# Loads in their order of use, an early table load and four products of zeros at the start of a decoder step on one core

## The chip, the core and the metric

The kernel runs on one core of a Trainium2 chip. Each engine works through its own list of instructions in order: TensorE (PE, with its weight loads as PEld), VectorE (DVE), ScalarE (ACT), GpSimd (POOL) and SyncE (SP), which here only issues loads and stores. An engine stops at an instruction until the semaphores that it waits for have come, and everything behind that instruction on the same engine stops too. The metric is the device time of one execution, in microseconds (us); lower is better.

## The reference, cut to what matters

One decoder layer takes a prompt of 1024 positions and 8 x 8 new positions of running sequences, 1088 columns of 1024 features in all. It has two parts, a token mixer (gated convolution, dilated attention, grouped attention) and a SwiGLU feed-forward network. Each part first norms its input and modulates it by a conditioning vector:

```
mod = silu(c) @ w_mod + b_mod              # c: 9 vectors of 1024; six groups of 1024 values
shift1, scale1, gate1, shift2, scale2, gate2 = split(mod, 6)
h   = rmsnorm(x, g_mix) * (1 + scale1) + shift1
... = h @ w_in                             # 1024 -> 2560 columns, read by all head groups
x   = x + gate1 * (mix @ w_out)
x   = x + gate2 * swiglu(rmsnorm(x, g_ffn) * (1 + scale2) + shift2, ...)
y   = rmsnorm(x, norm_final)
```

The change lies in the first microseconds of this: `silu(c)`, the first parts of `mod`, and the first projections of `h`.

## The kernel before

Data lie transposed: features on the 128 partitions, positions along the free dimension. So x is eight tiles x0 to x7 of 128 x 1088 (544 KB each), and the 1088 columns are worked in three groups of 366, 366 and 356. A product with full precision is made of three fast ones (lines 204, 205 and 206): every operand is cut into a high and a low part of the type fp32r, and high x high, high x low and low x high are added up in PSUM. For weights the cut is made in `halves` (line 90 on ACT for the high part, line 91 on DVE or POOL for the low part).

The start of the program is one long stage, in which four things run into each other:

- **The modulation.** `csil` is silu of the conditioning vectors (line 153, ACT). The weights `w_mod` come in tiles m0 to m23, four loads of 256 KB each. `mod_tile` (lines 173 to 197) makes two groups of four products of plain fp32 from such a tile (line 179; each of the four writes its own 32 of the 128 partitions). Then ACT copies the sum out of PSUM (`modev`, line 184), PE adds the four parts up by two small products (line 186), and DVE writes the result to `MOD` (lines 192 and 195). The tiles m0, m1, m2 and m3 give the scales of x0/x1, x2/x3, x4/x5 and x6/x7; m4 to m7 give the shifts. PSUM bank `t` serves m0 and m2, bank `o` serves m1 and m3; `o` has one buffer.
- **The scaled input.** For each of the eight x tiles ACT writes the high part of x times its scale (line 299) and DVE the low part (line 300), for three column groups.
- **The first two projections.** For each x tile PE makes 18 products (two blocks of weights x three column groups x three kinds), 144 in all, into six banks of PSUM that stay open for the whole stage. Their weights are w0 (for x0 to x3) and w1 (for x4 to x7), each two loads of 256 KB into `eraw`.
- **The norm.** ACT squares each x tile (lines 267 and 270), DVE or POOL adds the squares into `acc` (line 271), PE sums `acc` over the partitions (line 276, nine products of one column), a short chain on DVE and ACT makes the reciprocal root (lines 233 to 239), and PE spreads it over the partitions (line 282).

After line 282 the projections are scaled by the norm and the rest of the layer follows: further projections, attention, the decode part that streams the caches, the feed-forward network.

The order of the loads is written by hand, as a string of names at line 252; SP issues them in that order. At most eight loads of SP and ACT are under way, since they share eight semaphores. The order of the instructions on the other engines is not written by hand: a scheduler places them at build time by its own estimate of when each would be ready. When an input of that estimate changes (an arrival, an instruction more), it may place the instructions of all engines anew.

An fp32 product shows as two records in the trace, so that the four products of one group of line 179 are "x8" there and x4 in the program.

## Time and profile before

| what | value |
|---|---|
| three runs | 1392.35, 1392.99 and 1393.65 us, median 1392.99 us |
| the profiled execution: own time | 1396.23 us |
| the profiled execution: span, first to last instruction | 1394.2 us |
| busy share of PE over the span | 97% |
| mean granted clock of PE | 0.984 |
| share of PE in the chain that ended last | 88% |

The profiled execution is 3.2 us above the median of the runs, and its span is 2.0 us shorter than its own time. A timeline row gives the start in us from the span's start, the time in us, the engine, the line, the operation with what it writes and reads, and the count; in brackets the idle time before it and what ended that idle time. A row of windows gives for a stretch the busy time of each engine with its count of instructions, the granted clock of PE, the busy share of the DMA engines and GB/s.

### The profile page before, as it was taken

Reading aid. Unit: us, or ns where it says so; the run is one execution under the profiler, and the core shown is the slowest. Engines: PE = TensorE matmul, PEld = TensorE weight load, DVE = VectorE, ACT = ScalarE, POOL = GpSimd, SP = SyncE. Lnnn points to the kernel's source line nnn. Section 1 sums busy time; section 2 is a strip of 40 time slices with the busy share of each in tenths; the row PEclk is TensorE's granted clock in tenths of the full one; section 3 lists DMA queues with packets and bytes.
Section 4 is the critical chain, followed back from the end, with each engine's and each line's share of the span. In section 5 each row is a group of like instructions: output and inputs, shape, how many; then the busy total and the mean of one; then the engine's idle time right before and its main releaser. Section 6 shows DMA issues by size and latency. Waiting matters only on the chain.

```text
span 1394.2 us, 23856 instructions
## 1 busy us (share of the span) xinstructions
PE 1345.8 (97%) x9097; PEld 1281.3 (92%) x9097; DVE 850.7 (61%) x2016; ACT 596.0 (43%) x1227; POOL 199.1 (14%) x283
## 2 busy tenths in 40 slices
PE   7999999999999997999999999999999999999994
PEld 5889999988898886888999999999999999999994
DVE  4558868356676436325669766666666656566666
ACT  5488875466765324232345323232322222222252
POOL 2042310211101000000010111111111111111114
PEclk9999999999999998999999999999999999999996
DMA  9343431353406669775444413141423232323103
GB/s 362 111 154 100 144 100 32 122 183 107 145 24 228 225 237 333 249 297 182 115 136 123 128 61 91 57 155 61 153 90 129 88 125 91 122 92 121 52 23 129
DMA packets 77187, 190.90 MB, mean 137 GB/s; under 512 B 14048, under 2 KB 23808, under 8 KB 76288
## 3 DMA queue, kind: packets, MB, share of 16 engines
q1 hardware_dynamic: 73376, 135.67, 29.8%
q10 hardware_dynamic: 3536, 53.65, 10.7%
q8 instruction: 72, 1.18, 0.3%
q14 instruction: 43, 0.35, 0.1%
q0 software_dynamic: 160, 0.04, 0.0%
HBM read 181.32 MB, written 59.33 MB: 173 GB/s over the span
## 4 chain that ended last, share of the span: by engine, by line
PE 88%; DMA 4%; DVE 3%; ACT 2%; issue 2%; POOL 1%; SPq 0%; POOLq 0%; ACTq 0%; DVEq 0%
PE ps_g L204 20%; PE ps_g L206 19%; PE ps_g L205 19%; PE ps_s L205 3%; PE ps_s L204 3%; PE ps_s L206 3%; PE ps_o L582 3%; PE ps_t L204 2%; PE ps_t L205 2%; PE ps_t L206 2%; PE ps_t L573 2%; DMA wraw<-in_w_gu 2%; PE ps_s L529 1%; PE ps_s L530 1%; PE ps_g L179 1%
## 5 line engine op out<-in xcount | busy, mean ns | idle before, releaser
L204 PE MATMUL ps_g<-act,wsp 128*128 128x366 f32 (+1 forms) x1192 | 396.5, 334 | 2.2 <-DVE u L327 0.9
L205 PE MATMUL ps_g<-act,wsp 128*128 128x366 f32 (+1 forms) x1192 | 396.0, 332 | 0.0
L206 PE MATMUL ps_g<-act,wsp 128*128 128x366 f32 (+1 forms) x1192 | 392.9, 332 | 0.5 <-DVE wsp L91 0.3
L90 ACT ACTIVATE wsp<-wraw 128x512 fp32r<-128x512 f32 x232 | 145.8, 630 | 273.0 <-PE ps_g L206 174.9
L91 DVE TENSOR_TENSOR wsp<-wraw,wsp 128x512 fp32r<-128x512 f32 x232 | 167.2, 722 | 151.1 <-ACT wsp L90 145.5
L204 PEld LDWEIGHTS ps_g<-act,wsp 128*128 128x128 f32 x1192 | 225.3, 189 | 9.9 <-issue 3.3
L205 PEld LDWEIGHTS ps_g<-act,wsp 128*128 128x128 f32 x1192 | 225.7, 189 | 4.2 <-issue 2.3
L206 PEld LDWEIGHTS ps_g<-act,wsp 128*128 128x128 f32 x1192 | 224.7, 189 | 4.7 <-issue 3.1
L204 PE MATMUL ps_g<-hid,wsp 128*128 128x366 f32 (+3 forms) x464 | 153.6, 333 | 4.6 <-DVE ts L772 3.3
L205 PE MATMUL ps_g<-hid,wsp 128*128 128x366 f32 (+3 forms) x464 | 152.8, 329 | 1.5 <-DVE hid L857 1.4
L206 PE MATMUL ps_g<-hid,wsp 128*128 128x366 f32 (+3 forms) x464 | 153.1, 330 | 0.0
L204 PEld LDWEIGHTS ps_g<-hid,wsp 128*128 128x128 f32 x464 | 88.2, 190 | 7.8 <-DVE cv L768 3.8
L90 ACT ACTIVATE wsp<-tw 128x512 fp32r<-128x512 f32 x64 | 40.5, 633 | 122.2 <-PE ps_g L206 59.0
L205 PEld LDWEIGHTS ps_g<-hid,wsp 128*128 128x128 f32 x464 | 88.4, 191 | 2.3 <-DVE hid L857 2.1
L205 PE MATMUL ps_s<-act,wsp 128*128 128x366 f32 x272 | 90.2, 332 | 0.0
L204 PE MATMUL ps_s<-act,wsp 128*128 128x366 f32 x272 | 90.2, 331 | 0.0
L206 PE MATMUL ps_s<-act,wsp 128*128 128x366 f32 x272 | 90.0, 331 | 0.0
L206 PEld LDWEIGHTS ps_g<-hid,wsp 128*128 128x128 f32 x464 | 88.4, 190 | 0.0
L768 DVE SCALAR_TENSOR_TENSOR p_q<-ps_g,MOD,p_q 128x366 f32<-128x366 f32 (+3 forms) x99 | 55.4, 570 | 42.3 <-PE ps_g L206 42.2
L768 DVE SCALAR_TENSOR_TENSOR p_qc<-ps_g,MOD,p_qc 128x366 f32<-128x366 f32 (+3 forms) x99 | 56.5, 572 | 39.4 <-PE ps_g L206 37.6
L976 POOL TENSOR_TENSOR tw<-wraw 128x512 f32<-128x512 f32 x16 | 21.3, 1334 | 347.2 <-DMA wraw<-in_w_gu 209.5
L543 ACT ACTIVATE Sb<-Sb,st 128x257 f32<-128x257 f32 (+5 forms) x96 | 60.5, 632 | 21.1 <-DVE st L535 20.3
(337 smaller groups left out, 2319.3 us busy)
## 6 DMA issues: line engine op xcount, KB each, us to landing
wraw<-in_w_gu SPq DMA_DIRECT2D x112, 256.0 KB, 2.7
wraw<-in_wmod SPq DMA_DIRECT2D x64, 256.0 KB, 3.7
raw<-in_bk SPq DMA_DIRECT2D x30, 512.0 KB, 7.5
raw<-in_bv SPq DMA_DIRECT2D x30, 512.0 KB, 8.0
wraw<-in_w_in SPq DMA_DIRECT2D x36, 256.0 KB, 4.8
wraw<-in_w_d SPq DMA_DIRECT2D x36, 256.0 KB, 2.6
mraw<-in_wmod SPq DMA_DIRECT2D x32, 256.0 KB, 5.2
wraw<-in_w_out SPq DMA_DIRECT2D x32, 256.0 KB, 2.7
```

Source lines behind the costliest of these rows:

```text
L90: S.activation(sp[:, 0, :], raw, AF.Copy)
L91: (V if not state["sub"] or state["n"] % state["sub"] else G).tensor_tensor(sp[:, 1, :], raw, sp[:, 0, :].bitcast(F32), op=OP.subtract)
L179: ins = PE.matmul(ps[32 * q:32 * q + 32, :256], lhsT=csil[:, 4 * hf + q, :], rhs=raws[2 * hf + q // 2][:, q % 2 * 256:q % 2 * 256 + 256], ...
L204: PE.matmul(ps[:, :n], lhsT=w_hi, rhs=a(0, ak), start=first and j == 0, stop=False, **kw)
L205: PE.matmul(ps[:, :n], lhsT=w_hi, rhs=a(1, ak), start=False, stop=False, **kw)
L206: PE.matmul(ps[:, :n], lhsT=w_lo, rhs=a(0, ak), start=False, stop=last and j == m - 1, **kw)
L529: PE.matmul(ps[:, :sn], lhsT=QH[:, qsl], rhs=KS[hd][:, kk], start=True, stop=False)
L543: S.activation(Sb[:, :ne], Sb[:, :ne], AF.Exp, scale=-1.0, bias=m, accum_out=st[:, 3:4])
L573: PE.transpose(pt[:, col:col + 128], Sb[:, (kb - k0) * 128:(kb - k0 + 1) * 128], ident)
L582: PE.matmul(po[:, q0:q0 + w], lhsT=Vt[:, kb, hd].rearrange("p a b -> p (a b)"), rhs=PT[:, hl, c0:c0 + w], start=fresh, stop=ch is chunks[- ...
L768: ins = V.scalar_tensor_tensor(x1[m][:, c0:c0 + k], ps[:, :k], MOD[:, gate + m, 0:1], x1[m][:, c0:c0 + k], op0=OP.mult, op1=OP.add)
L976: G.tensor_tensor(t1, b12, b11, op=OP.subtract)
```

## The change

It has three parts.

1. A tile `warm` of 128 x 256 is set to zero by DVE, and ACT runs Silu on one column of `ones` into its first column, ahead of the instruction that makes `csil`. The table of Silu, which ACT loads before the first instruction that needs it, is so loaded ahead of that instruction; before, the load stood behind the wait for `cT`, the conditioning vectors.
2. Four fp32 products of 128 x 128 by 128 x 256 of that tile lead on PE, into bank `o`, whose values nobody reads. They read the whole tile, the column that ACT writes too, so they wait for ACT's Silu.
3. The loads of the start come in another order.

```
+WARM = 4
 ...
     csil = cse.tile([128, KC, 32], F32, name="csil")
     V.memset(csil, 0.0)
+
+    warm = stp.tile([128, 256], F32, name="warm")
+    V.memset(warm, 0.0)
+    S.activation(warm[:, 0:1], ones, AF.Silu)
+    pw = ps_tile("o")
+    for i in range(WARM):
+        PE.matmul(pw[:, :256], lhsT=warm[:, 128:256], rhs=warm, start=True, stop=True)
     S.activation(csil[:, :, 0:9], cT, AF.Silu)
 ...
-    for item in "m0 w0 m1 x0 x1 m2 x2 m3 x3 x4 w1 x5 x7 x6 m4 m5 m6 m7".split():
+    for item in "m0 x0 w0 x1 m1 x2 x3 m2 x4 w1 x5 m3 x6 x7 m4 m5 m6 m7".split():
```

The lines behind the insertion have numbers higher by 2, then by 9: line 90 becomes 92, 179 becomes 188, 184 becomes 193, 186 becomes 195, 204 to 206 become 213 to 215, 276 becomes 285, 299 becomes 308.

The scheduler answers with another order on every engine in the first 50 us. Beyond, a stretch of some 200 instructions on PE between the last attention and the first decode steps differs in the places of single products, and so do two instructions at the end: the last group's norm is begun by line 233 on DVE and line 234 on ACT, and these now stand behind the three multiplications of line 1077 (DVE) and behind two stores of the output (ACT). Everything else keeps its order.

First place: SP, the very first loads (`mraw` are the tiles m, `eraw` w0 and w1, x_82 to x_89 are x0 to x7). Before:

```order
L97 DMA mraw<-in_wmod 128x512 x4
L97 DMA eraw<-in_w_in 128x512 x2
L97 DMA mraw<-in_wmod 128x512 x4
L257 DMA x_82<-in_xT 128x1088
L257 DMA x_83<-in_xT 128x1088
L97 DMA mraw<-in_wmod 128x512 x4
L257 DMA x_84<-in_xT 128x1088
L97 DMA mraw<-in_wmod 128x512 x4
L257 DMA x_85<-in_xT 128x1088
L257 DMA x_86<-in_xT 128x1088
```

Now:

```order
L99 DMA mraw<-in_wmod 128x512 x4
L266 DMA x_82<-in_xT 128x1088
L99 DMA eraw<-in_w_in 128x512 x2
L266 DMA x_83<-in_xT 128x1088
L99 DMA mraw<-in_wmod 128x512 x4
L266 DMA x_84<-in_xT 128x1088
L266 DMA x_85<-in_xT 128x1088
L99 DMA mraw<-in_wmod 128x512 x4
L266 DMA x_86<-in_xT 128x1088
L99 DMA eraw<-in_w_in 128x512 x2
L266 DMA x_87<-in_xT 128x1088
L99 DMA mraw<-in_wmod 128x512 x4
```

x0 has moved ahead of w0 and m1, and m3 from ahead of x3 to behind x5.

Second place: ACT, from the table load on. Before:

```order
L153 ACT_TABLE_LOAD
L153 ACTIVATE csil<-cT 128x8x9
L90 ACTIVATE wsp<-eraw 128x512
L184 ACTIVATE modev<-ps_t 128x256
L90 ACTIVATE wsp<-eraw 128x512
L184 ACTIVATE modev<-ps_o 128x256
L299 ACTIVATE act<-x_82,MOD 128x366 x2
```

Now:

```order
L158 ACT_TABLE_LOAD
L158 ACTIVATE warm<-ones 128x1
L162 ACTIVATE csil<-cT 128x8x9
L276 ACTIVATE acc_228<-x_82 128x1088
L92 ACTIVATE wsp<-eraw 128x512 x2
L193 ACTIVATE modev<-ps_t 128x256
L308 ACTIVATE act<-x_82,MOD 128x366 x2
```

The copy of m0's sum (`modev<-ps_t`) has moved behind the square of x0 and behind both conversions of w0.

Third place: PE, where m3 is made (`ps_o<-mraw`). Before, after four of its products further up:

```order
L179 MATMUL ps_o<-mraw,csil 32x256
L205 MATMUL ps_g<-act,wsp 128x366
L206 MATMUL ps_g<-act,wsp 128x366
L205 MATMUL ps_s<-act,wsp 128x366
L206 MATMUL ps_s<-act,wsp 128x366
L179 MATMUL ps_o<-mraw,csil 32x256
L204 MATMUL ps_g<-act,wsp 128x356
L204 MATMUL ps_t<-act,wsp 128x356
L179 MATMUL ps_o<-mraw,csil 32x256 x2
L186 MATMUL ps_t<-sel,modev 128x9 x2
L205 MATMUL ps_g<-act,wsp 128x356
```

Now, for its second group of four:

```order
L213 MATMUL ps_t<-act,wsp 128x356
L214 MATMUL ps_t<-act,wsp 128x356
L215 MATMUL ps_t<-act,wsp 128x356
L188 MATMUL ps_o<-mraw,csil 32x256 x4
L195 MATMUL ps_o<-sel,modev 128x9 x2
L285 MATMUL ps_o<-ones,acc_228 128x1 x9
L213 MATMUL ps_g<-act,wsp 128x366
L213 MATMUL ps_s<-act,wsp 128x366
```

The pieces of m3 have become whole groups of four, and the second group, the two products of line 186 (now 195) that need its copy from ACT, and the nine of line 276 (now 285) follow each other with no other product between them; before, other products stood between these three.

## The prediction

> **What bounds the kernel now.** I read the page first: who is busy, and when.
>
> ```profile
> PE 1345.8 (97%) x9097; PEld 1281.3 (92%) x9097; DVE 850.7 (61%) x2016; ACT 596.0 (43%) x1227; POOL 199.1 (14%) x283
> PE   7999999999999997999999999999999999999994
> ```
>
> TensorE works nearly all the time, so a microsecond taken from its list is a microsecond gained, and one that is put in is lost. The change touches the first slice, which has a 7. Two windows of that stretch, and rows of PE's timeline in it, come next.
>
> ```profile
> 10.00:20.00 10.00, 9.18 (x46) 6.21 (x47) 6.78 (x19) 7.53 (x15) 0.51 (x1) 1.00 1.04 402
> 13.74:48.35 34.61, 34.61 (x203) 29.75 (x204) 25.11 (x59) 24.34 (x48) 6.40 (x3) 1.00 0.84 307
> 8.70 1.02 PE L186 MATMUL ps_t<-sel,modev 128*128 128x9 f32 x4 [0.61 <-ACT modev L184]
> 9.88 1.08 PE L179 MATMUL ps_o<-mraw,csil 128*32 128x256 f32 x8 [0.15 <-DMA mraw<-in_wmod]
> 13.74 0.65 PE L204 MATMUL ps_g<-act,wsp 128*128 128x366 f32 x1
> 48.35 0.83 PE L282 MATMUL ps_o<-ident,ir_y 128*128 128x128 f32 x6
> ```
>
> The second row matters most: from the first projection product at 13.74 us to line 282 at 48.35 us PE is busy 34.61 of 34.61 us. Before 13.74 it waits for loads and makes the tiles m0 and m1 meanwhile, so these cost nothing. The time can only fall if the dense stretch begins earlier, holds less work or runs at a faster pace.
>
> Its pace is not even:
>
> ```profile
> 15.10 0.51 PE L205 MATMUL ps_g<-act,wsp 128*128 128x366 f32 x1
> 15.40 0.51 PE L206 MATMUL ps_g<-act,wsp 128*128 128x366 f32 x1
> 17.84 0.50 PE L204 MATMUL ps_t<-act,wsp 128*128 128x356 f32 x1
> 19.28 0.43 PE L205 MATMUL ps_g<-act,wsp 128*128 128x356 f32 x1
> 20.71 0.33 PE L205 MATMUL ps_g<-act,wsp 128*128 128x366 f32 x1
> 20.88 0.33 PE L206 MATMUL ps_g<-act,wsp 128*128 128x366 f32 x1
> ```
>
> A product starts every 0.305 us until 17.84 and every 0.167 us from 19.28 on. The granted clock reads 1.00 in the window from 10 to 20 us above, so it does not show this first slow stretch; the spacing does. The 14 products from 13.74 to 17.84 lose 14 x 0.138 = 1.9 us.
>
> **The table load.** Before:
>
> ```profile
> 3.95 1.28 ACT L153 ACT_TABLE_LOAD   x1 [3.95 <-DMA cT<-in_cT]
> 5.24 0.27 ACT L153 ACTIVATE csil<-cT 128x72 f32<-128x72 f32 x1
> 7.01 1.08 PE L179 MATMUL ps_t<-mraw,csil 128*32 128x256 f32 x8 [0.37 <-DMA mraw<-in_wmod]
> ```
>
> Now the load can run from 2.1 us, when ACT's three DMA issues are over, and `csil` is ready at about 4.2 instead of 5.5. But the second group of m0 starts at 7.01 on its own load, not on `csil`. The gain is zero.
>
> **The zeros.** They wait for ACT's Silu, so they start at about 3.6. Each fills the array as the four products of a group of line 179 do together, and such a group takes 1.08 us at the slow pace, a little less in a stream; four zeros take about 3.8 us (estimate from that row). They end near 7.4, when m0's last load has landed. Cost: at most 0.4 us on m0, covered by ACT's queue below. PE then works without a pause from 3.6 to about 9.4. What they may buy is the fast pace; see the rivals.
>
> **The start of the dense stretch.** It needs x0, w0 and m0's scale.
>
> ```profile
> 12.60 0.23 DVE L296 TENSOR_TENSOR tsx<-x,MOD 128x64 f32<-128x64 f32 x1 [2.06 <-DMA x<-in_xT]
> 9.82 0.48 DVE L192 TENSOR_SCALAR MOD<-ps_t,biasT,gT 128x9 f32<-128x9 f32 x2 [0.64 <-ACT wsp L90]
> 12.71 1.51 ACT L299 ACTIVATE act<-x,MOD 128x366 fp32r<-128x366 f32 x3
> 14.11 1.10 ACT L267 ACTIVATE acc<-x 128x1088 f32<-128x1088 f32 x1
> 8.55 0.62 ACT L90 ACTIVATE wsp<-eraw 128x512 fp32r<-128x512 f32 x1
> 8.28 0.37 ACT L184 ACTIVATE modev<-ps_t 128x256 f32<-128x256 f32 x1
> ```
>
> x0 landed at 12.5 us. At 402 GB/s (the window 10 to 20) a load of 256 KB takes 0.65 us; x0 now passes six of them (w0 and m1), so it lands near 12.5 - 3.9 = 8.6, and w0 at 9.3 and 9.9. This looks like 4 us gained, but ACT's queue takes most of it back: the square of x0 (1.10) and both conversions of w0 (0.62 each) stand ahead of m0's copy. 8.6 + 1.1 = 9.7, two conversions to 10.9, copy to 11.25. Before, line 186 began at 8.70 and its first result could be used about 1.4 later (9.82 plus one of the two writes). So line 299 starts at 12.65 and the first product at 13.2: **0.5 us gained**.
>
> **What the dense stretch holds now.** m1's two groups and its line 186 ran in the idle time before; now they stand inside. m3 was scattered over single products, now it is two whole groups.
>
> ```profile
> 27.05 0.32 PE L206 MATMUL ps_t<-act,wsp 128*128 128x356 f32 x1
> 27.30 0.63 PE L179 MATMUL ps_o<-mraw,csil 128*32 128x256 f32 x6
> 27.86 0.44 PE L204 MATMUL ps_g<-act,wsp 128*128 128x366 f32 x1
> 29.14 0.33 PE L204 MATMUL ps_s<-act,wsp 128*128 128x366 f32 x1
> 29.41 0.62 PE L179 MATMUL ps_o<-mraw,csil 128*32 128x256 f32 x2
> 29.95 0.43 PE L205 MATMUL ps_g<-act,wsp 128*128 128x366 f32 x1
> 33.66 0.54 PE L186 MATMUL ps_o<-sel,modev 128*128 128x9 f32 x4
> ```
>
> Three products of line 179 take 27.86 - 27.05 - 0.167 = 0.64 us out of the stream, and a single one takes 29.95 - 29.14 - 0.167 = 0.64 as well: the four of a group run side by side, and a piece costs the same however few are in it. Line 186 takes about 0.5 (33.66). So m1 adds 2 x 0.64 + 0.5 = **1.8 us**; m3 loses its three pieces too many, of which one lay beside m2's group and cost about a half, 2.5 x 0.64 = **1.6 us** less.
>
> **New waits.** Before, the trace shows none in this stretch. Now PE's list has three places where a result is used right behind its making. (a) m1's line 186, one group of m2, then the products of x2: write of MOD, line 299 and PE's start need about 1.45 us from line 186's start, the work between fills 1.1; wait 0.4. (b) m2's line 186 after only four products of x2, while ACT makes three of line 299 (1.51) and the copy (0.37) first; wait 0.4. (c) m3's second group, copy, line 186, then line 276, which writes the one buffer of bank `o` and waits for DVE's reading of it: 0.2 + 0.37, then 0.3; together 0.9. Sum **1.7 us**, between 0 (each result there in time) and 2.7 (a full microsecond more for ACT being late).
>
> Order and waits together: -0.5 + 1.8 - 1.6 + 1.7 = **+1.4 us**. This takes the slow pace at the start as equally long after the first product.
>
> **A fall of the pace at (c).** Two places in the trace show the clock fall after a thin stretch, and one shows it hold:
>
> ```profile
> 63.60:67.00 3.40, 2.48 (x29) 1.70 (x27) 0.86 (x5) 0.48 (x2) 0.27 (x2) 1.00 0.00 0
> 67.00:70.40 3.40, 3.39 (x30) 3.02 (x31) 0.32 (x2) 0.83 (x4) 0.13 (x1) 0.51 0.00 0
> 364.00:367.40 3.40, 2.24 (x19) 1.46 (x19) 3.22 (x10) 3.34 (x8) 0.00 (x0) 1.00 0.87 270
> 367.40:370.80 3.40, 3.40 (x16) 3.40 (x17) 3.14 (x11) 3.36 (x7) 0.00 (x0) 0.50 0.42 151
> 43.38 2.06 PE L276 MATMUL ps_o<-ones,acc 128*128 128x1 f32 x18
> ```
>
> With 2.48 and 2.24 us of 3.40 busy the next 3.4 us run at half clock. The 2.06 us of one-column products at 43.38 alone did not do it. Now (c) makes group, wait, line 186, wait and line 276 follow each other: 0.64 + 0.57 + 0.5 + 0.3 + 1.9 = 3.9 us without a projection product, thinner than 63.60 to 67.00. I hold a fall for likely. Price: 3.4 us at half pace are 11 products instead of 20, 9 x 0.167 = 1.5 us, less where part of it falls on line 276; I take **+1.0**, bounds 0 and 3.0 (two such windows).
>
> The Trainium skill (TensorE: Matmul & The Clock Gate, "The HAM clock gate") gives that clock a window of about 3.4 us, free-running: one busy window releases it, an idle one halves it. The 3.4 us at 0.51 agree. Its table "Why this matters for your kernels" asks for no idle gap over about 3 us; by that no fall comes at (c), where the longest gap is 0.6 us. The row 63.60 speaks against it.
>
> **Further on.** Between 440 and 472 us, where single products are swapped, PE is full, so the swaps cost nothing, give or take 0.5. At the end the norm waits behind line 1077 today:
>
> ```profile
> 440.00:472.00 32.00, 32.00 (x295) 28.75 (x298) 15.25 (x43) 12.09 (x27) 4.15 (x18) 1.00 0.58 194
> 1379.90 0.52 ACT L1070 ACTIVATE rs<-ps_s 128x416 f32<-128x416 f32 x1 [1.78 <-PE ps_s L806]
> 1380.54 0.16 DVE L233 TENSOR_SCALAR ir_v<-ps_t 128x2 f32<-128x2 f32 x1 [1.83 <-PE ps_t L802]
> 1380.62 0.64 DVE L1077 SCALAR_TENSOR_TENSOR cv<-cv,gT,ps_s 128x416 f32<-128x416 f32 x1
> 1382.29 0.16 DVE L235 RECIPROCAL ir_y<-ir_y 128x2 f32<-128x2 f32 x1
> ```
>
> Their input is there at 1379.9, so in front of line 233 they end at 1381.6 instead of 1382.3; line 233 and ACT's root follow to about 1382.0: **-0.3**, no worse than +0.3.
>
> **Sum.** +1.4 + 1.0 - 0.3 = +2.1 us. The profiled execution's own time, 1396.23, would become 1398.3; it lies 3.2 above the median of the runs. On the median 1392.99 it gives **1395.1 us**.
>
> **Rivals.** *The order alone* (the clock holds at (c)): +1.4 - 0.3, 1394.1. For it: the longest gap there is short. Against: row 63.60.
>
> *The zeros bring the full pace and it lasts.* Then the 1.9 us of the first products, about 0.4 on m1's group and 0.5 on line 186 go. The square of x4 stands on ACT ahead of x2's scaling and waits for x4 (near 20.8: m3's four loads less and one x more than x3 before, at 22.0), so PE's products of x2 can't start before 22.5. In the forecast they start at 13.2 + 36 x 0.167 + 2.3 of slow pace + four groups at 0.64 + 0.5 + wait 0.4 = 25.0, so the gain is at most 2.5: 1.4 - 2.5 - 0.3, 1391.6. For it: 5.8 us of unbroken work; by the skill's budget of about 3.4 us (same page) that suffices. Against: then comes a pause of some 2 us and another of 1 us around a thin line 186, thinner than the rows that lost the clock.
>
> *Faster:* the full pace and no wait at (a), (b), (c), because the scheduler's estimate was right: 1391.6 - 1.7, 1389.9. Against: ACT's chain above.
>
> *Slower still:* the pace falls at (a)-(b) and at (c), each time for two windows: 1.4 + 4 x 1.0 - 0.3, 1398.1. It decides once the waits at (a) and (b) together exceed the 0.9 us idle of the stretch at 63.60.
>
> **How the numbers follow.** Forecast 0.41, order alone 0.25, full pace 0.14, faster 0.06, slower still 0.14. About 0.2% or 2.8 us is what a measurement here tells from no change. Slower by that: the last case, and the part of the forecast with over a full window of half clock, 0.16: 0.30. Faster by that: 0.06 and a part of the full pace, 0.03: 0.09. Within: 0.61. The range runs from just under the full pace to the last case, 1391.2 to 1398.0; the forecast's own is 1393.5 to 1397.
>
> **What would show it.** Line 299's first row near 12.6 and the first product near 13.2; the copy of m0 behind two conversions; waits of PE for ACT's `modev` before lines 195 and 285; half clock in the window behind line 285; line 282's twin later than 48.35. I am wrong if products are 0.167 apart from the first on, if the first stands before 12.5, or if line 282's twin comes earlier than 48.

## The result: slower by 10 us, and the profile after

| | before | after |
|---|---|---|
| median of the runs (eight each) | 1393.10 us (1389.29 to 1399.17) | 1403.36 us (1398.92 to 1407.47) |
| ratio, 95% interval | 1 | 1.0069 (1.0050 to 1.0088) |
| the profiled execution, own time | 1396.23 us | 1401.78 us |
| its span | 1394.2 us | 1399.7 us |

The change makes the kernel slower. The direction was the one forecast, the size was not: 1395.1 was forecast, with a range that ended at 1398.0. The two profiled executions differ by 5.5 us only, since that of before lies 3.1 above its median and that of after 1.6 below. The first rows of after's page:

```profile
PE 1345.0 (96%) x9105; PEld 1282.2 (92%) x9105; DVE 853.3 (61%) x2017; ACT 595.9 (43%) x1228; POOL 201.8 (14%) x283
PE   7999999999999997999999999999999999999994
PEclk9999999999999998999999999999999999999998
```

and the clock's row on the page of before:

```profile
PEclk9999999999999998999999999999999999999996
```

The sums of busy time are those of before within 3 us on every engine, so what has grown is the time in which PE waits. PE's sum could stay the same, although products at half clock take longer, because this execution of before had half clock elsewhere: in its last slice the clock reads 6, in that of after 8. Rows of PE's timeline of after, in the order of the steps of the prediction:

```profile
3.71 3.77 PE L161 MATMUL ps_o<-warm 128*128 128x256 f32 x8 [3.71 <-ACT warm L158]
7.42 1.07 PE L188 MATMUL ps_t<-mraw,csil 128*32 128x256 f32 x16
10.84 1.02 PE L195 MATMUL ps_t<-sel,modev 128*128 128x9 f32 x4 [2.35 <-ACT modev L193]
12.94 0.67 PE L213 MATMUL ps_g<-act,wsp 128*128 128x366 f32 x1 [1.07 <-ACT act L308]
13.40 0.51 PE L213 MATMUL ps_s<-act,wsp 128*128 128x366 f32 x1
13.84 1.08 PE L188 MATMUL ps_o<-mraw,csil 128*32 128x256 f32 x8
14.85 0.68 PE L213 MATMUL ps_g<-act,wsp 128*128 128x366 f32 x1
24.93 0.43 PE L213 MATMUL ps_g<-act,wsp 128*128 128x366 f32 x1 [0.52 <-ACT act L308]
34.75 0.44 PE L214 MATMUL ps_g<-act,wsp 128*128 128x366 f32 x1 [1.16 <-DVE act L309]
37.97 0.44 PE L214 MATMUL ps_g<-act,wsp 128*128 128x366 f32 x1 [1.11 <-DVE act L309]
39.05 0.43 PE L214 MATMUL ps_g<-act,wsp 128*128 128x356 f32 x1 [0.48 <-DVE act L313]
43.63 0.61 PE L195 MATMUL ps_o<-sel,modev 128*128 128x9 f32 x4 [0.59 <-ACT modev L193]
44.98 3.97 PE L285 MATMUL ps_o<-ones,acc 128*128 128x1 f32 x18 [0.74 <-DVE tsx L305]
56.18 0.83 PE L291 MATMUL ps_o<-ident,ir_y 128*128 128x128 f32 x6
```

Down to 24.93 this is the forecast (25.0), in part by luck: the first product is 0.3 us earlier than forecast and fewer products run slowly, while m1's pieces cost more. Then come three waits for DVE, of 1.16, 1.11 and 0.48 us, that no step of the prediction names. Line 285 takes 3.97 us where it took 2.06, and the twin of line 282, the marker of all that follows, starts at 56.18 instead of 48.35: 7.8 us late.

What DVE does ahead of those waits, and POOL beside it (after):

```profile
12.91 3.00 DVE L309 SCALAR_TENSOR_TENSOR act<-x,MOD,act 128x366 fp32r<-128x366 f32 x6
30.34 8.52 DVE L309 SCALAR_TENSOR_TENSOR act<-x,MOD,act 128x366 fp32r<-128x366 f32 x6
28.89 2.62 POOL L93 TENSOR_TENSOR wsp<-eraw,wsp 128x512 fp32r<-128x512 f32 x1 [17.03 <-DMA mraw<-in_wmod]
31.46 5.62 POOL L280 TENSOR_TENSOR acc<-acc,sq 128x1088 f32<-128x1088 f32 x2
```

Six low parts take 3.00 us at 12.91, and 8.52 at 30.34, where POOL's low part of w1 and both of its adds of squares run at the same time. The profile of before holds the same thing once, small and without harm:

```profile
37.79 2.61 POOL L271 TENSOR_TENSOR acc<-acc,sq 128x1088 f32<-128x1088 f32 x1 [6.32 <-ACT sq L270]
39.17 2.57 DVE L300 SCALAR_TENSOR_TENSOR act<-x,MOD,act 128x366 fp32r<-128x366 f32 x3 [1.18 <-ACT act L299]
42.87 1.53 DVE L300 SCALAR_TENSOR_TENSOR act<-x,MOD,act 128x366 fp32r<-128x366 f32 x3
```

Three low parts took 2.57 us beside POOL's add and 1.53 without it. The Trainium skill (SBUF — State Buffer, "SBUF: two separate sides") says that DVE and GpSimd share a pair of ports which goes to one instruction as a whole, while the other engine waits (on DVE's side for one with two inputs in SBUF, as the low part has). The trace agrees: the first of the three took 1.63 us, until 0.4 us behind the end of POOL's add, and the other two took 0.59 and 0.51. So an instruction of DVE waits for the end of the one on POOL; the two do not share in proportion.

Windows of after: the whole dense stretch, and three windows of 3.41 us around line 285 (busy time of PE, PEld, DVE, ACT and POOL, then the granted clock):

```profile
12.94:56.18 43.24, 38.55 (x223) 32.76 (x223) 29.69 (x58) 24.11 (x48) 8.11 (x3) 0.87 0.71 254
41.49:44.90 3.41, 2.16 (x18) 1.36 (x17) 0.59 (x5) 0.61 (x2) 0.00 (x0) 1.00 0.74 190
44.90:48.31 3.41, 3.33 (x16) 3.36 (x16) 2.26 (x6) 3.39 (x9) 0.00 (x0) 0.50 0.34 124
48.31:51.72 3.41, 3.41 (x14) 3.41 (x14) 2.19 (x10) 1.10 (x2) 0.00 (x0) 0.50 0.00 0
```

Before, the stretch was 34.61 us with PE busy all the time; now it is 43.24 with 38.55 busy. The fall of the clock behind (c) is there, after a window with 2.16 us busy, and lasts two windows.

Behind the start the two profiled executions run like this (start of the same instruction, in us):

| | before | after | late by |
|---|---|---|---|
| line 282, its twin 291 | 48.35 | 56.18 | 7.8 |
| first product of line 701, its twin 710, of 500 us | 500.33 | 505.60 | 5.3 |
| the same line near 546 | 545.97 | 552.40 | 6.4 |
| the same line near 633 | 633.26 | 642.69 | 9.4 |
| line 707, its twin 716, near 642 | 642.06 | 652.79 | 10.7 |
| line 802, its twin 811, near 1356 | 1355.91 | 1365.44 | 9.5 |
| end of the span | 1394.2 | 1399.7 | 5.5 |

The 2.5 us regained by 500 us go with two windows of half clock that this execution of before had, and after's had not (from 67.0 and 367.4 us); one of after's own (from 434.0) gives a little of it back. At 1356 us the difference is 9.5, close to the 10.3 of the medians. The 4.0 us that come back at the end go with the clock: it is at half from 1367.5 us to the end in before, and from 1386.3 us in after. So 5.5 us says too little of the change, and the medians say it better. The 5.5 us lost between 500 and 652 go with two waits for loads of the caches and the half clock behind them (rows of before, then of after):

```profile
545.97 0.64 PE L701 MATMUL ps_o<-raw,PTs 128*32 128x128 f32 x16 [1.52 <-DMA raw<-in_bv]
633.26 0.65 PE L701 MATMUL ps_o<-raw,PTs 128*32 128x128 f32 x16 [1.74 <-DMA raw<-in_bv]
```

```profile
552.40 0.64 PE L710 MATMUL ps_o<-raw,PTs 128*32 128x128 f32 x16 [2.74 <-DMA raw<-in_bv]
553.74 0.51 PE L213 MATMUL ps_g<-act,wsp 128*128 128x366 f32 x1
554.04 0.51 PE L214 MATMUL ps_g<-act,wsp 128*128 128x366 f32 x1
642.69 1.08 PE L710 MATMUL ps_o<-raw,PTs 128*32 128x128 f32 x16 [2.38 <-DMA raw<-in_bv]
```

Behind 552.40 the products are 0.305 us apart, and line 710 at 642.69 takes 1.08 instead of 0.65: half clock after both waits.

### The profile page after: what moved, and what is told of

It is laid out like the page before. It is cut to its first block, busy times and chain, and to the rows that moved or that the text cites. A ratio compares the mean times of both kernels' runs of the same rounds, so it can differ in the third digit from the quotient of the medians.

```text
span 1399.7 us, 23879 instructions
## 1 busy us (share of the span) xinstructions
PE 1345.0 (96%) x9105; PEld 1282.2 (92%) x9105; DVE 853.3 (61%) x2017; ACT 595.9 (43%) x1228; POOL 201.8 (14%) x283
## 3 DMA queue, kind: packets, MB, share of 16 engines
q10 hardware_dynamic: 3536, 53.65, 10.7%
## 4 chain that ended last, share of the span: by engine, by line
PE 88%; DMA 4%; DVE 3%; ACT 2%; issue 1%; POOL 1%; SPq 0%; POOLq 0%; ACTq 0%; DVEq 0%
PE ps_g L213 19%; PE ps_g L215 19%; PE ps_g L214 19%; PE ps_s L214 3%; PE ps_s L213 3%; PE ps_s L215 3%; PE ps_o L591 3%; PE ps_t L214 2%; PE ps_t L213 2%; PE ps_t L215 2%; PE ps_t L582 2%; DMA wraw<-in_w_gu 2%; PE ps_s L538 1%; PE ps_s L539 1%; DMA raw<-in_bv 1%
## 5 line engine op out<-in xcount | busy, mean ns | idle before, releaser
L213 PEld LDWEIGHTS ps_g<-hid,wsp 128*128 128x128 f32 x464 | 87.1, 188 | 8.6 <-DVE cv L777 4.8
L214 PEld LDWEIGHTS ps_g<-hid,wsp 128*128 128x128 f32 x464 | 87.3, 188 | 0.3
L215 PEld LDWEIGHTS ps_g<-hid,wsp 128*128 128x128 f32 x464 | 87.3, 188 | 0.0
```

Of the source, the lines that this page charges most:

```text
L213: PE.matmul(ps[:, :n], lhsT=w_hi, rhs=a(0, ak), start=first and j == 0, stop=False, **kw)
L214: PE.matmul(ps[:, :n], lhsT=w_hi, rhs=a(1, ak), start=False, stop=False, **kw)
L215: PE.matmul(ps[:, :n], lhsT=w_lo, rhs=a(0, ak), start=False, stop=last and j == m - 1, **kw)
```

## The experiments

The marker in this table is the start of line 282 or its twin (48.35 before). "Total" is the ratio to the kernel before, less one, times 1393, with its 95% interval; each run is compared with runs of the kernel before from its own session (medians 1391.57 to 1394.13 us), 6 to 12 runs of it against 22 or more, the change with eight against eight. "Waits" are PE's waits for the loads of bv near 546 and 636 us, a star where half clock follows.

| run | marker, us | total, us | waits, us |
|---|---|---|---|
| before | 48.35 | 0 | 1.52, 1.74 |
| the change | 56.18 | +9.6 (7.0 to 12.3) | 2.74*, 2.38* |
| e1 order of loads alone | 51.66 | +2.0 (-0.1 to 4.2) | 1.87, 1.21 |
| e2 zeros and early Silu alone | 52.82 | +7.7 (5.2 to 10.0) | 2.45*, 2.65* |
| e3 the change, adds on DVE | 55.10 | +5.9 (3.1 to 8.6) | 2.59*, 3.74* |
| e4 before, adds on DVE | 49.72 | +0.1 (-2.0 to 2.4) | 1.70, below 0.4 |
| e5 early Silu alone | 47.65 | +0.8 (-1.5 to 3.3) | 2.10, 0.81 |
| e6 zeros alone | 46.60 | -0.6 (-3.3 to 2.2) | 1.13, 1.28 |
| e7 order, adds on DVE | 46.79 | -1.5 (-3.8 to 0.8) | 2.57*, 1.15 |
| e8 as e7, m3 earlier | 44.93 | -2.9 (-5.2 to -0.7) | 2.40*, 1.64 |
| e9 the change, zeros in the thin stretch | 56.80 | +14.1 (10.7 to 17.4) | 2.45*, 2.24* |
| e10 before, 12 zeros at 54 us | 47.91 | +8.9 (6.0 to 11.8) | 2.32*, 2.11* |
| e11 the change without early Silu | 53.00 | +6.0 (4.0 to 8.1) | 0.99, 1.52 |
| e12 as e8, zeros between | 44.63 | +1.0 (-1.3 to 3.3) | 1.96, 1.80 |
| e13 before, 14 zeros at 54 us | 48.11 | +8.6 (5.9 to 11.4) | 0.32, 1.12 |
| e14 before, 4 zeros at 54 us | 47.60 | +4.0 (2.1 to 6.0) | 1.92, 3.16* |
| e15 the change, zeros of 192 columns | 52.62 | +7.4 (4.5 to 10.3) | 1.50, 3.17* |
| e16 as e8, m2 earlier too | 46.06 | +0.1 (-2.2 to 2.5) | 2.00, 1.34 |

### The halves of the change, and POOL's adds

e1 changes the string of the loads in the kernel before and nothing else:

```
-    for item in "m0 w0 m1 x0 x1 m2 x2 m3 x3 x4 w1 x5 x7 x6 m4 m5 m6 m7".split():
+    for item in "m0 x0 w0 x1 m1 x2 x3 m2 x4 w1 x5 m3 x6 x7 m4 m5 m6 m7".split():
```

> The new order of the loads alone: no zeros, no early Silu. Marker: the start of line 282 (48.35 us in the kernel before; its twin 291 at 56.18 in the changed one). Theory A (the loss is made of two things that the new order brings: DVE and POOL take turns, so that DVE's low parts stand behind POOL's two adds of squares and PE waits 2.7 us for them, and a half clock of about 3 us behind the thin stretch around line 276): the copy of m0 is no longer queued behind the square of x0 and two conversions, so the first product comes near 10.7 instead of 12.94, but PE still waits 2.5 to 2.8 us for line 300 while POOL adds, and line 276 takes about 4 us again; marker 50.5 to 53, total 2 to 6 us above before. Theory B (the zeros and the early Silu are what costs): marker 47 or earlier, total at or below before.

e2 is the changed kernel with the old string, so it has the zeros and the early Silu alone.

> The zeros and the early Silu alone, with the loads in the order of before. Theory A: what matters is only whether the instructions, placed anew, put POOL's two adds beside six low parts of DVE. Here they do (both adds follow the low part of w1 on POOL), so PE waits 2 us or more for line 309 and the marker (line 291) is at 53 to 55, total 5 to 9 us above before. Theory B (the order of the loads is what costs, the lead costs nothing): no wait of PE for line 309, marker 48 to 49, total within 2 us of before.

e3 is the changed kernel with this line altered, and e4 the kernel before with it:

```
-ACCE = tuple("vvvvvggv")
+ACCE = tuple("vvvvvvvv")
```

> The changed kernel with all adds of squares on DVE, none on POOL. Theory A: the waits of PE for line 309 (1.16 and 1.11 us) and 313 (0.48) go, although DVE has two adds (2.5 us) more to do; the six low parts take 3.0 us instead of 8.52. The thin stretch around line 285 stays, and so may the half clock there. Marker (line 291) 52 with a half clock at line 285, 49 without, against 56.18; total 3 to 5 us less than the changed kernel. Rival C (x4, x5 or their scales are late, and POOL's adds only stand beside it): waits for line 309 of 2 us or more remain, marker 55 or later.

> Control: the kernel before with all adds of squares on DVE. Theory A: there POOL's adds met DVE in one instruction only (1.63 us instead of 0.59), which cost PE nothing, and DVE has room; marker (line 282) 47.8 to 49, total within 2 us of before. If adds on DVE are better or worse by themselves, whatever stands beside them, the total moves by as much as in the changed kernel (3 to 5 us less).

e7 has both: the new string in the kernel before, and the adds on DVE.

> The new order of the loads without zeros and Silu, and the adds of squares on DVE, none on POOL. Theory A (DVE and POOL take turns, and PE waits for DVE): against the order alone, whose marker was 51.66, the wait for line 304 (1.57 us) goes and the six low parts take 3.0 us: marker 45.5 to 48, total 0 to 3 us less than before. Rival: x6 and x7 or the scales of m3 are late as well, so the wait only moves to lines 299 or 186; marker 50 or later, total 1 to 3 us above before.

Rows of DVE and PE of e1:

```profile
30.77 8.09 DVE L300 SCALAR_TENSOR_TENSOR act<-x,MOD,act 128x366 fp32r<-128x366 f32 x5
39.04 0.44 PE L205 MATMUL ps_g<-act,wsp 128*128 128x356 f32 x1 [1.57 <-DVE act L304]
51.66 0.83 PE L282 MATMUL ps_o<-ident,ir_y 128*128 128x128 f32 x6
```

and of e7:

```profile
29.39 3.53 DVE L300 SCALAR_TENSOR_TENSOR act<-x,MOD,act 128x366 fp32r<-128x366 f32 x5
46.79 0.83 PE L282 MATMUL ps_o<-ident,ir_y 128*128 128x128 f32 x6
```

The two differ in POOL's adds alone (and in what the scheduler made of that). Five low parts take 8.09 us beside them and 3.53 without, PE's wait of 1.57 is gone, and the marker comes 4.9 us earlier, though DVE has two adds of about 1.3 us more to do. Not all of the 4.9 is the wait: e7's first product comes at 10.77 and e1's at 11.49, and e1 has a window of half clock behind line 276 (45.2 to 48.6) that e7 has not, worth some 1.5 us. By total e7 stands 3.5 below e1, with intervals that just overlap. Two details of e1 came otherwise than expected: the wait was 1.57 us and not 2.5 to 2.8, and line 276 took 2.14 and not about 4, since the clock fell behind it. e3 says the same of the changed kernel: the waits for lines 309 and 313 are gone, and from x2's first product to the marker it takes 55.10 - 26.77 = 28.3 us instead of 56.18 - 24.93 = 31.3. Its marker was still not the 52 expected: in that execution the first stage was 1 us later, and PE stayed at half clock until 20.5 us. The six low parts took 4.03 us and not 3.0, with POOL's low part of w1 beside the first (3.81 us, 1.26 alone). The total, 3.7 less than the change, lies in the 3 to 5 expected, but the two intervals overlap. e4 is the control: where POOL's adds met DVE once only, moving them gained nothing (the marker is even 1.4 us later). That POOL's adds keep DVE from its low parts, and so PE from its products, is shown by the rows; how much of the total that is, is not.

But the order of the loads, alone, costs 2.0 us only, with no certain difference from zero; the zeros and the early Silu, alone, cost 7.7. In e2, too, PE waits for DVE, but only in part because of POOL, whose adds run from 33.50 to 36.34 and from 36.84 to 39.35:

```profile
33.50 2.84 POOL L280 TENSOR_TENSOR acc<-acc,sq 128x1088 f32<-128x1088 f32 x1 [1.80 <-ACT act L312]
33.88 2.54 DVE L313 TENSOR_TENSOR act<-tsx,act 128x64 fp32r<-128x64 f32 x1
34.01 0.60 PE L215 MATMUL ps_g<-act,wsp 128*128 128x366 f32 x2 [1.89 <-DVE wsp L93]
36.48 0.66 PE L214 MATMUL ps_g<-act,wsp 128*128 128x356 f32 x1 [0.86 <-DVE act L313]
```

The instruction of line 313 takes 0.21 us elsewhere; here it took 2.54 and ended 0.08 us behind POOL's add. PE's wait of 0.86 is for it, and a third one, 0.55 at 39.80, is for a low part beside the second add. The wait of 1.89 is none of POOL's: it began at 32.11, ahead of the add, and ended with DVE's low part of w1, which took its usual 0.68 us behind an add of DVE's own. A wait of 1.75 at the marker, for the end of the norm's chain on DVE, is another that no run takes apart. So the scheduler's order costs in e2 by more ways than POOL. Nor does every meeting cost: in e11 POOL's adds stand beside low parts too (six took 5.28 us), and no wait of PE for a low part in e11 is longer than 0.43.

### The halves of the lead

e5 leaves the zeros out of e2, e6 the early Silu; e11 leaves the early Silu out of the changed kernel; e15 makes the changed kernel's zeros shorter:

```
# e5
-    pw = ps_tile("o")
-    for i in range(WARM):
-        PE.matmul(pw[:, :256], lhsT=warm[:, 128:256], rhs=warm, start=True, stop=True)
# e6, e11
-    S.activation(warm[:, 0:1], ones, AF.Silu)
# e15
-        PE.matmul(pw[:, :256], lhsT=warm[:, 128:256], rhs=warm, start=True, stop=True)
+        PE.matmul(pw[:, :192], lhsT=warm[:, 128:256], rhs=warm[:, :192], start=True, stop=True)
```

> The early Silu alone: no zeros, loads in the order of before. PE's list is that of before, instruction for instruction. Theory D (the lead costs through the new placing of the start and through something that four more products on PE shift further on; the Silu has no part in it): marker (start of line 282's twin) 48.35 give or take 0.6, no half clock between 545 and 660 us, waits of PE for the loads of bv of 1.2 to 1.9 us, total within 2 us of before. Rival E (the Silu costs, since it stands ahead of other work on ACT): marker 50 or later, total 4 us or more above before.

> The zeros alone: no early Silu, loads in the order of before; the zeros now run before 6 us and PE's list behind them is nearly that of before. In the two kernels with zeros profiled so far, two waits of PE for the loads of bv (near 552 and 642 us) are 2.4 to 2.7 us and each is followed by one window of half clock (3.4 us), while in the kernels without zeros they are 0.4 to 1.9 us and no half clock follows; this is worth about 5 us. Theory D (four more products on PE bring that, whatever the start looks like): marker 48 to 49, but the two waits and the two half windows are there, total 4 to 6 us above before. Rival E (the start alone brings it, by the time at which the later stages meet the loads): marker 48 to 49, no half window between 545 and 660, total within 2 us of before.

> The changed kernel without the early Silu: the zeros wait for the setting of their tile only and run from about 1.5 us, the loads are in the new order. Theory G (zeros that wait for ACT's Silu are what turns the order of the start: the square of x0 and two conversions come ahead of the copy of m0): the first product comes at 11 to 12.2 instead of 12.94, waits for DVE of about 1.5 us and a half clock near line 285 stay as in the order alone; marker 50.5 to 53, total 1 to 4 us above before. Rival (order and zeros together cost, gated or not): marker 55 or later, total 7 us or more above before.

> The changed kernel with zeros of 192 columns instead of 256, everything else as it is. The scheduler places the start and the stretch from 430 to 500 us otherwise for it: the copy of m0 stands ahead of the second conversion of w0, m3's second group lies apart from line 285, and the middle is that of the kernel before. Theory P (the loss of the changed kernel is one of placing, not of the zeros' work or of the early table load): first product at 11.9 to 12.7, marker 50.5 to 53.5 instead of 56.18, no half clock between 540 and 660 us, total 2 to 6 us above before instead of 10. Rival (zeros behind the early Silu and the new order of loads cost 10 us together, however placed): marker 55 or later, total 8 us or more above before.

Each half alone costs nothing that can be told (+0.8 and -0.6, both with zero inside). So the zeros' work and the early table load are as cheap as the prediction said. Theory D, that four products more on PE cause the later loss, falls with e6: no half clock there. With the loads in the old order it is the two together that cost: zeros that wait for Silu end at 7.5 instead of 5.3 us, and the scheduler, which estimates this, places the start anew, as the lists of the instructions show. e15 shows how little that takes. With 192 columns instead of 256 the same instructions come in another order: the copy of m0 ahead of the second conversion of w0, m3's second group apart from line 285. The marker falls from 56.18 to 52.62, as expected, though the first product came at 13.06 and not by 12.7. The total falls by 2.2 only, to 7.4, between what theory and rival gave, and the two intervals overlap. e11's marker of 53.00 lies in what its theory gave, its total of 6.0 between theory and rival, and its first product at 12.49, after the 12.2 expected. With the new order of loads, zeros without the early Silu thus cost as well.

### The clock

e9 puts four products of zeros next to the two waits of (c); e12 takes e8 and puts zeros where PE waits ahead of the first product:

```
# e9, in mod_tile for m3 alone; a second pair of the same lines stands behind line 195's products
+        if t == 3:
+            with tc.issue_after(ins.ins):
+                for i in range(2):
+                    PE.matmul(ps[:, 288:512], lhsT=warm[:, 128:256], rhs=warm[:, :224], start=True, stop=True)
# e12, ZER = (6, 2, 2): six at the start, two between m0's second group and line 186, two behind line 186
+    zeros(ZER[0])
...
+        if t == 0:
+            with tc.issue_after(ins.ins):
+                zeros(ZER[1])
```

> The changed kernel with four more products of zeros at the place of waiting around line 285: two between the second group of m3 and line 195, two between line 195 and line 285 (128x128 by 128x224, about 0.4 us each at full pace, 1.7 us in all, where PE waits 0.59 and 0.74 now). Theory (the stretch loses the clock since too few columns stream through PE in it): no half clock at line 285, its eighteen records take 2.06 us instead of 3.97, the products behind it start 0.167 us apart; marker (line 291's twin) 56.18 + 0.4 - 3.2 = 53.4, total 2 to 4 us less than the changed kernel. Rival (the one-column products of line 285 lose the clock whatever stands ahead of them, or it fell by chance): half clock as before, marker 56.5 to 57, total as the changed kernel or above.

> The run with the adds on DVE and m3 ahead of x4 (marker 44.93, 3.4 us below before), with products of zeros that wait for nobody but their tile: six at the start, two between m0's second group and line 186, two behind line 186, where PE waits for ACT. Theory (the slow pace of the first products comes from too few columns streaming before them): products 0.167 us apart from the first or second on, the first at 11.3 to 12.2 instead of 10.73; marker 43 to 44.5, total 1 to 3 us less than that run. Rival (the pace is regained and lost again before the first product, as in the changed kernel): products 0.305 apart until 15, marker 45 to 46.5, total that of that run or 1 to 2 us above it.

In e9 the zeros did not fill the waits. They write into m3's own bank, so that the first two stand behind the same wait for ACT's copy as line 195 does (0.59 us), and the wait of line 285 is still 0.74 us behind the second two. What e9 tests is therefore only whether more streaming products in that stretch hold the clock. Rows and two windows of e9 (line 293 is the twin of 285):

```profile
42.67 1.02 PE L197 MATMUL ps_o<-warm 128*128 128x224 f32 x4 [0.59 <-ACT modev L193]
43.90 1.00 PE L204 MATMUL ps_o<-warm 128*128 128x224 f32 x4
43.33:46.74 3.41, 2.67 (x20) 2.35 (x20) 1.52 (x6) 1.41 (x3) 0.00 (x0) 1.00 0.42 148
46.74:50.15 3.41, 3.41 (x16) 3.41 (x16) 2.70 (x9) 3.31 (x8) 0.00 (x0) 0.50 0.02 5
45.63 2.96 PE L293 MATMUL ps_o<-ones,acc 128*128 128x1 f32 x18 [0.74 <-DVE tsx L313]
```

The fall came all the same, one step later and again for two windows, and the total is 4.5 us above the change (the intervals overlap). In e7, 2.83 of 3.41 us around line 276 kept the clock; here 2.67 lost it, and in e1 even a window with 3.12 busy did (41.78 to 45.19, with line 276 in it), while before kept it behind one with 1.67 (630.23 to 633.64). So the busy share of PE's rows does not say when it falls, and why it falls there stays open. The runs do show where. In six of the 18 (the change, e1, e3, e9, e11 and e15) the row of line 186 for m3 begins 1.2 to 2.1 us ahead of line 276, and the clock falls at the start of line 276, in it, or 1 us behind it. In the other twelve it begins 2.8 us or more ahead, and the clock holds through line 276. It is not enough to take m3's groups of four away (e1, e11 and e15 have them 9 us ahead); in e8 the groups and line 186 both stand over 10 us ahead.

At the start, zeros do what they are meant to, if they stand in the waits themselves (e12):

```profile
12.11 0.43 PE L221 MATMUL ps_g<-act,wsp 128*128 128x366 f32 x1
13.36 0.33 PE L223 MATMUL ps_g<-act,wsp 128*128 128x366 f32 x1
13.53 0.33 PE L222 MATMUL ps_s<-act,wsp 128*128 128x366 f32 x1
13.70 0.33 PE L223 MATMUL ps_s<-act,wsp 128*128 128x366 f32 x1
44.63 0.91 PE L299 MATMUL ps_o<-ident,ir_y 128*128 128x128 f32 x6
```

The first five steps between products are 0.22 to 0.27 us and the next ones 0.167; none has the 0.305 of the half clock. But the first comes at 12.11 instead of 10.73 in e8: m0's groups wait until the first zeros end at 6.99, and PE then waits 1.11 us more for the copy by ACT. The marker gains 0.3, and the total stands 3.9 above e8, not 1 to 3 below. In the changed kernel the clock was full at 7.35 and half again from 10.76 to 17.59: its zeros ended at 7.48, and the wait of 2.35 us for the copy followed.

### The later loss

e10, e13 and e14 leave the start of before as it is and add nothing but work of known size behind line 282:

```
     rrow = first_rstd()
+    warm = stp.tile([128, 256], F32, name="warm")
+    V.memset(warm, 0.0)
+    pw = ps_tile("o")
+    for i in range(LATE):        # e10: 12, e13: 14, e14: 4
+        PE.matmul(pw[:, :256], lhsT=warm[:, 128:256], rhs=warm, start=True, stop=True)
```

> The kernel before with twelve products of zeros put on PE near 60 us, behind line 282: 12 x 0.47 = 5.6 us more work there, the start untouched. What is in question is the stretch from 545 to 650 us, where the profiled executions with a late start (the changed kernel, the lead alone, the adds on DVE) lose 5 us more, by two waits for loads of bv of 2.4 to 3.7 us, each with half clock behind it. Theory L (a late start makes these later waits longer): the two waits are 2.4 us or more, half clock follows them, total 8 to 12 us above before. Rival (the later loss belongs to these kernels' own order of instructions, or to chance): waits of 0.4 to 1.9 us there, total 3.5 to 6 us above before.

> As the kernel before with twelve zeros near 60 us, with fourteen: 14 x 0.445 = 6.2 us of work, the start untouched. With fourteen the order of the single products between 430 and 500 us is that of the kernel before; with twelve it was that of the changed kernel. Theory O (this order decides whether the waits for bv near 545 and 640 us grow beyond 2.3 us and half clock follows): waits of 0.4 to 2.1 us, no half clock between 540 and 660, total 4 to 7 us above before, less than the 9.1 of the twelve. Theory L (lateness decides): both waits 2.3 us or more, half clock behind both, total 9 to 13 us above before.

> As the run before it, with four zeros: 1.8 us of work, the start untouched, and between 430 and 500 us the order of the changed kernel. Theory O: the wait for bv near 545 us is 2.3 us or more and half clock follows it, total 2.5 to 6 us above before, more than its zeros cost. Theory L: waits below 2.2 us, no half clock between 540 and 660 us, total 0 to 2.5 us above before.

The zeros took 5.34, 6.21 and 1.89 us, and the totals rose by 8.9, 8.6 and 4.0: each time by 2 to 4 us more than they take (only e13's interval reaches down to its zeros' own time). Work put in early thus costs more than its own time in this kernel, be it by lateness or by what the scheduler makes of it. How, the traces do not settle. The waits of e13, then of e14:

```profile
549.26 0.65 PE L707 MATMUL ps_o<-raw,PTs 128*32 128x128 f32 x16 [0.32 <-DMA raw<-in_bv]
636.31 0.64 PE L707 MATMUL ps_o<-raw,PTs 128*32 128x128 f32 x16 [1.12 <-DMA raw<-in_bv]
```

```profile
544.81 0.64 PE L707 MATMUL ps_o<-raw,PTs 128*32 128x128 f32 x16 [1.92 <-DMA raw<-in_bv]
633.77 0.65 PE L707 MATMUL ps_o<-raw,PTs 128*32 128x128 f32 x16 [3.16 <-DMA raw<-in_bv]
```

e13 is late and has short waits; e14 is hardly late and has a long one, at the second place. So lateness alone does not make these waits long (e11 speaks against it too), and neither does the order of the products between 430 and 500 us alone: e15 has that of before and a wait of 3.17. Both theories fall as sole causes. Since one execution stands behind each pair of waits, and the times of one kernel spread over 5 to 14 us, the loads' chance in the single execution may be a good part of it; that is argued, not shown.

### A version that may beat both

e8 loads m3 ahead of x4, without zeros and early Silu and with all adds on DVE; e16 also loads m2 ahead of x3:

```
# e8
+    for item in "m0 x0 w0 x1 m1 x2 x3 m2 m3 x4 w1 x5 x6 x7 m4 m5 m6 m7".split():
# e16
+    for item in "m0 x0 w0 x1 m1 x2 m2 x3 m3 x4 w1 x5 x6 x7 m4 m5 m6 m7".split():
```

> As the run before it in this list, with m3 loaded ahead of x4 instead of behind x5, so that its two groups and line 186 lie apart from line 276. Theory A with the thin stretch at line 276: no half clock within 10 us behind line 276, and no wait of PE above 1 us between its first projection product and line 282; marker 44 to 46, total 1 to 5 us less than before. Rival (the later stages take back whatever the start gains, since they wait for the loads of the caches): marker as said, total within 1 us of before.

> A version meant to beat both: no lead, all adds of squares on DVE, loads m0 x0 w0 x1 m1 x2 m2 x3 m3 x4 w1 x5 x6 x7, that is m2 ahead of x3 and m3 ahead of x4. Start as in the run with m3 ahead of x4 (marker 44.93), and between 430 and 500 us the order of the kernel before. Theories A and O: marker 44.5 to 45.5, no half clock between 540 and 660 us, total 3 to 6 us below before. Rival (what the start gains is given back by the later stages whatever their order): total within 2 us of before.

e8's first product stands at 10.73 and its marker at 44.93; no wait above 1 us follows, and the clock holds through line 276. Its ratio to before is 0.9979 (0.9963 to 0.9995): about 3 us faster, at the edge of what can be told, and 12.5 us less than the change. e16 did not repeat it: its first product came at 11.72, a microsecond later than in e8, its marker was 46.06, outside the 44.5 to 45.5 expected, and its total is that of before, as its rival said. With one interval of sixteen runs that just leaves zero out on the fast side, e8's gain over before may be chance; its gain over the change is not.

## Why the prediction was wrong, step by step

**Right.** The table load gained nothing and the zeros' own work cost nothing that can be told (e5, e6). The first product came at 12.94 (forecast 13.2) behind the copy that two conversions hold up, with a wait of 2.35 us. The pace was slow at first, the zeros notwithstanding. x2's first product came at 24.93 (25.0), in part by luck, as said above. Wait (a) was 0.52 us (0.4). The waits ahead of lines 195 and 285 and the half clock behind them came where the text put them. The rival of a full pace that lasts failed for the reason given there.

**The step that failed first** is "New waits", whose sum was 1.7 us with an upper bound of 2.7. Measured: (a) 0.52, (b) 0.09, (c) 0.59 + 0.74 = 1.33, and 1.16 + 1.11 + 0.48 = 2.75 at three places that the step does not name; 4.69 in all, which is 43.24 - 38.55. The bounds were drawn for ACT being late. That DVE can be late because POOL works was not among them, and the sum put it at nothing without a reason, though the trace of before had the row (2.57 us for three low parts, 1.53 elsewhere), and though the new order showed both of POOL's adds in a row beside six low parts. e3 shows that this is the cause: without POOL's adds these three waits are gone; e7 against e1 says the same.

**The second** is "A fall of the pace at (c)": +1.0 with an upper bound of 3.0. The mechanism came, at 3.15: line 285 took 3.97 instead of 2.06, and ten products behind it stood 0.305 instead of 0.167 apart for nine steps (1.9 + 1.25). The text took line 276 as a discount on the price, "less where part of it falls on line 276". Its products took nearly twice as long like all others, and they stood on the path.

**Smaller terms.** m1's pieces cost 2.35 instead of 1.8: the first group ran at the slow pace (14.85 - 13.40 - 0.305 = 1.15), the second took 0.65, line 195 took 0.55. The start gained 0.8 instead of 0.5. With m3's 1.6 as forecast, -0.8 + 2.35 - 1.6 + 4.7 + 3.15 = 7.8, and the marker is 7.8 late. The forecast had 2.4. That the sum closes is in part luck. The slow pace was taken as equally long, but 11 products ran slowly instead of 14 and m2's first group cost 0.65 instead of 1.14, some 0.9 us less; about as much is gone again at the waits, since a product with a wait behind it takes 0.33 us and one in the stream 0.167.

**The third step** is "Further on", where the swaps were to cost nothing, give or take 0.5. The profiled execution of after lost 5.5 us (10.73 - 5.27) between 500 and 652 us. Whether the swaps have a part in it is open; e13 to e15 show that they do not decide it alone. What e10, e13 and e14 show is that work put in early costs 2 to 4 us beyond itself (e13's interval allows none), which no term of the sum held. The tail's -0.3 cannot be told from the clock of that stage.

**What the sum took for granted** was that a part that costs nothing by itself may be left out of the account. The zeros and the early Silu, one by one, cost nothing that can be told, and 7.7 us together; the scheduler gave the two together another order, and no run splits the 7.7 into its parts.

## What to carry to other kernels

Where a change gives a scheduler a new order, look not only for what waits for whom but for which instructions of VectorE and GpSimd will run side by side: an add that hides on GpSimd may take the time of the low part for which TensorE waits. Zeros brought TensorE's full pace to the first real products only where they filled the waits up to these (e12), and there they held up the small products on which the first one depends; in no run did the total clearly gain by them. A part that costs nothing alone should be tried together with the others, since four short products moved everything here; and the totals, not the first stage, should decide, since 1.9 to 6.2 us of work put in early cost 4.0 to 8.9 in the end.

## What the runs showed of the hardware

- DVE and POOL stop one another for whole instructions. A DVE instruction of 0.21 us took 2.54 beside POOL's add and ended 0.08 us behind it (e2). Six low parts (128x366, some 128x292) took 3.00 us alone and 8.52 beside three instructions of POOL, five took 3.53 without its adds and 8.09 with them. POOL's low part of 128x512 took 1.26 alone, 2.62 beside DVE.
- How long a pause the clock bears is not one number. In 18 profiled executions, all 14 of PE's waits for loads of bv near 546 and 636 us that were 2.11 us or longer were followed by half clock, and none of the 22 of up to 2.10 us was. Elsewhere it came otherwise: in e7 a pause of 1.61 us at 862.8 was followed by half clock from 865.6, and in the change one of 3.17 us at 1374.7 by none until 1386.3. The Trainium skill (TensorE: Matmul & The Clock Gate, "Why this matters for your kernels") asks for no idle gap over about 3 us; here pauses of 1.61 and of 2.11 to 3.74 us were followed by half clock, and one of 3.17 was not.
- Around the products of one column, without a pause over 0.8 us, the clock fell after windows with 2.16 (the change), 2.67 (e9) and 3.12 us (e1) busy of 3.41, and held with 2.83 (e7): the busy share does not decide it. Full clock came at 7.35 in the changed kernel, after zeros from 3.71 on, and was gone by 10.76, after a wait of 2.35 us.
